# Second layer's keys of a two-layer encoder trunk: block turns on VectorE and 256-byte-run stores in place of transposes on TensorE

## The chip, the cores and the metric

One core of one Trainium2 chip runs the whole program in one launch. The metric is device time in microseconds (us); three runs of the kernel before give a median of 1708.25 us (1708.22 to 1708.37). The engines are TensorE (PE in the profile; PEld is its weight load), VectorE (DVE), ScalarE (ACT), GpSimd (POOL) and SyncE (SP). In this kernel POOL and SP mostly issue transfers.

## The reference

Two request groups, x_prompt and x_sample, of 512 tokens by 1024 numbers each, go through the same two layers: differential attention, then bidirectional retention, each with a SiLU gate and a residual, and a last norm. All is float32. What matters here is the second layer's mixer, cut to its core:

```python
def bidir_retention(h, w_in, decay_fwd, decay_bwd, subln_g, w_out):
    proj = h @ w_in
    q, k, v, gate = jnp.split(proj, [...], axis=-1)
    q = retention_rotate(q.reshape(B, S, N_HEADS, RET_QK_DIM))
    k = retention_rotate(k.reshape(B, S, N_HEADS, RET_QK_DIM)) * (RET_QK_DIM ** -0.5)
    log_g_f = -jnp.exp(decay_fwd)
    log_g_b = -jnp.exp(decay_bwd)
    o_f = retention_direction(q, k, v, log_g_f, True)
    o_b = jnp.flip(retention_direction(jnp.flip(q, 1), jnp.flip(k, 1), jnp.flip(v, 1), log_g_b, False), 1)
    o = rms_norm(o_f + o_b, subln_g, SUBLN_EPS)
    o = o.reshape(B, S, D_INNER) * jax.nn.silu(gate)
    return o @ w_out
# in retention_direction, for each chunk of tokens:
    scores = jnp.einsum('bqhd,bkhd->bhqk', qc, kc) * intra[None]
    state = (state * chunk_decay + jnp.einsum('bkhd,bkhe->bhde', kc * k_decay, vc))
```

There are 8 heads; a key of the second layer has 128 numbers, a value 256.

## The kernel before, in words

**Numbers.** A float32 operand is split into a high part (the float32r rounding, by ACT, `hi_of`, L534) and a low part (the rest, by DVE, `lo_of`, L537), and a product is three matmuls. The projections are done in blocks of seven products in place of eight (`Unit`, matmuls L752, and `Double`, for the values, with the operands changed over, matmuls L887; L1197 are the output projections').

**Stages.** Norm and first layer's projections, attention, its output projection, norm and second layer's projections (about 1060 to 1410 us of the span), retention (about 1410 to 1685 us), output projection, last norm. Both groups go through each stage. Between projections and mixers the rotated q and k, the values, the gates and the turned keys lie in HBM (`qk_d`, `v_d`, `g_d`, `kt_d`; qk, v, g and kt in the profile), stored by POOL's queue (L530) from the staging ring `os` and loaded by SP's queue.

**Keys of the second layer.** The projection leaves q and k with the head's 128 numbers along partitions and 512 tokens along the free axis. A unit holds a pair of heads. `rot_done` rotates its two halves into two tiles (an m and an e buffer), splits and stores them, and for keys calls `turn`, eight times in all (four pairs, two groups). The retention's state needs the keys the other way, tokens along partitions, multiplied by powers of the decay. `turn` (L968 to L993) turns each of the two tiles with four transposes on PE into a PSUM bank (L978, ring tp, one buffer), takes them out with two multiplies by `powers` (L982, DVE), and splits and stores two heads' keys of 512 KB each, high and low. In the retention, `fetch2` loads a block (one head of one group): q, k, values, turned keys (both parts, into the arena) and gate; L1784 are the state's products, of turned keys and values, twelve matmuls a block.

**What sets the order.** The program's operations are listed once, with what each reads and writes, in the class `Plan`; `arrange` puts them in an order by a list of costs and due times, per engine, and `issue` writes that order out. `SHIFTS` is a table of numbers, each row a place in time, a reach, a size, a share and a seed, which moves due times at random before each arrangement; so the table sets the order. Buffers come from rings: `os` 3, e 8, m 4, c 4, ws (split weights) 7; PSUM banks pj 3, sc 2, o 2, tp 1. An operation that writes a ring's next buffer waits for the last readers of the one before in that place, a store among them.

Of the kernel before, what the change touches and what calls it, by code (L numbers as in the profile page):

```python
# [10 lines left out]
F32 = mybir.dt.float32  # L11
# [71 lines left out]
class Buf:  # L83
# [37 lines left out]
    (1423.43, 30, 2, 0.05, 47590),
    (11.99, 16, 0.3, 0.05, 523605),
    (1423.39, 30, 1, 1, 258131),
    (542.13, 8, 2, 0.5, 679735),
    (11.49, 16, 0.3, 1, 785172),
    (1415.16, 30, 4, 0.05, 143263),
    (1052.6, 30, 2, 0.5, 712630),
    (1425.39, 30, 1, 0.5, 612061),
    (1421.39, 16, 2, 0.5, 937799),
    (1440.0, 16, 4, 0.2, 433253),  # L130
    (1432.0, 8, 2, 0.2, 226625),
    (1439.5, 16, 2, 0.5, 224311),
    (167.17, 30, 0.3, 1, 538302),
    (60.85, 8, 4, 0.2, 501862),
    (971.85, 16, 2, 0.2, 92752),
# [227 lines left out]
def trunk_kernel(  # L363
# [84 lines left out]
    def const(shape, tag, dt=F32, size=None):  # L448
        return Buf(plan, tag, 1, lambda i: view(cp, tag, i, size or math.prod(shape[1:]), shape, dt))
# [130 lines left out]
    powers = const([P, NH, NT], "powers")  # L580
# [344 lines left out]
    def rot_done(dst, tab, scaled, turned=None, weave=woven):  # L925
# [14 lines left out]
        def store(g, i, r):  # L940
# [29 lines left out]
        def turn(g, *r):  # L970
            h, to = turned
            out = [m_t("kt"), m_t("kt")]
            for i in range(2):
                tp = bank("tp", "ktp")

                def fn(i=i, tp=tp):
                    for t in range(NT):
                        nc.tensor.transpose(  # L978
                            tp[:, t * P:(t + 1) * P], unwoven(r[i].t)[:, t // 2, t % 2 * P:(t % 2 + 1) * P], ident.t)
                pe(0.44, fn, [r[i], ident], [tp], 2)  # L980
                for j in range(2):
                    dve(256, lambda i=i, j=j, tp=tp: nc.vector.tensor_tensor(  # L982
                        out[j].t.rearrange("p (t i c) -> p t i c", t=NT, i=2)[:, :, i, :],
                        tp.t.rearrange("p (t j c) -> p t j c", t=NT, j=2)[:, :, j, :],
                        powers[:, h + j, :].unsqueeze(2).broadcast_to([P, NT, 64]), op=ALU.mult),
                        [tp, powers], [(out[j], i)])
# [1031 lines left out]
```

## Time and profile before

| | |
|---|---|
| median of 3 runs | 1708.25 us |
| profiled execution's time | 1708.25 us |
| its span | 1706.5 us |
| PE busy | 1695.6 us (99%) |
| PEld busy | 1504.9 us (88%) |
| DVE busy | 1478.3 us (87%) |
| ACT busy | 906.1 us (53%) |
| POOL busy | 359.5 us (21%) |
| chain that ended last | PE 94%, DVE 4%, issue 1%, POOL 1% |

The span reaches from the first to the last instruction of the profiled execution; the time has 1.75 us more around it. In a group's row stand the line, the engine, the operation, output<-inputs by the program's names, shapes and count, then the busy time in us and the mean of one in ns, then the engine's idle time ahead of them and what ended it. In the waits a row names who waited for whom, us in total, times, and the longest. In the table of stretches the columns are the stretch, its length, then busy us and instructions of PE, PEld, DVE, ACT and POOL, the granted clock, the transfers' share and GB/s.

### The profile page before, as it was taken

The page shows a single profiled execution, that of the slowest core. Times are in us where ns is not written, and L with a number is a line of the kernel's source. Part 1 is how long each engine was busy: PE and PEld are TensorE (multiplying, and loading weights), DVE is VectorE, ACT ScalarE, POOL GpSimd, SP SyncE. Part 2 cuts the span into 40 slices and gives each one's busy share as a digit, 9 for nine tenths or more (in the row PEclk, how much of TensorE's full clock was granted, in tenths as well). Part 3 has the DMA queues.
Part 4 walks back from the last instruction along what each step waited for, and adds up shares of the span by engine and source line. Part 5 has one row for each costly group of instructions (what it writes and reads, how often), then busy time and mean ns, then how long its engine had stood idle before and what let it go on. Part 6 is the DMA issues. An engine that isn't in the chain of part 4 may idle for free.

```text
span 1706.5 us, 24879 instructions
## 1 busy us (share of the span) xinstructions
PE 1695.6 (99%) x8729; PEld 1504.9 (88%) x8729; DVE 1478.3 (87%) x2394; ACT 906.1 (53%) x1863; POOL 359.5 (21%) x656
## 2 busy tenths in 40 slices
PE   9999999999999999999999999999999999999998
PEld 8888888888888899888888988888888889999997
DVE  8978979989579889898888898877996797998988
ACT  8754444444444565555555876454544455544446
POOL 1111242222232212111111201124222321111114
PEclk9999999999999999999999999999999999999999
DMA  5344664556455795554443525456565569765652
GB/s 224 136 148 145 198 239 161 173 163 197 156 215 173 240 365 185 198 196 172 159 176 150 198 69 185 168 183 236 167 218 192 214 215 406 286 246 194 251 205 99
DMA packets 100469, 337.02 MB, mean 197 GB/s; under 512 B 14052, under 2 KB 15224, under 8 KB 100344
## 3 DMA queue, kind: packets, MB, share of 16 engines
q1 hardware_dynamic: 66992, 226.02, 36.7%
q0 software_dynamic: 33024, 109.08, 18.7%
q8 instruction: 68, 1.11, 0.3%
q14 instruction: 57, 0.47, 0.1%
q10 hardware_dynamic: 328, 0.34, 0.1%
HBM read 217.94 MB, written 117.44 MB: 197 GB/s over the span
## 4 chain that ended last, share of the span: by engine, by line
PE 94%; DVE 4%; issue 1%; POOL 1%; ACT 0%; DMA 0%; POOLq 0%; DVEq 0%; ACTq 0%
PE pj L752 20%; PE pj L1197 18%; PE sc L752 10%; PE o L752 8%; PE pj L887 7%; PE sc L1464 5%; PE o L887 4%; PE sc L887 4%; PE o L1538 3%; PE o L1805 3%; PE tp L887 2%; PE o L1585 2%; PE o L1813 1%; PE sc L1760 1%; PE tp L1784 1%; PE pj L1505 1%
## 5 line engine op out<-in xcount | busy, mean ns | idle before, releaser
L1197 PE MATMUL pj<-ws,arena 128*128 128x512 f32 x1542 | 359.1, 381 | 0.1
L1197 PEld LDWEIGHTS pj<-ws,arena 128*128 128x128 f32 x1542 | 283.9, 190 | 35.8 <-DVE m L1012 0.3
L752 PE MATMUL pj<-b,ws 128*128 128x512 f32 x1080 | 251.2, 380 | 1.1 <-DVE e L813 0.6
L752 PEld LDWEIGHTS pj<-b,ws 128*128 128x128 f32 x1080 | 203.5, 189 | 30.0 <-DVE e L813 1.0
L1203 DVE SCALAR_TENSOR_TENSOR b<-pj,pad,b 128x512 f32<-128x512 f32 (+1 forms) x257 | 190.1, 743 | 11.5 <-PE pj L1197 10.7
L537 DVE TENSOR_TENSOR ws<-raw,ws 128x512 fp32r<-128x512 f32 (+2 forms) x173 | 152.3, 884 | 41.9 <-PE tp L887 21.5
L530 POOL DMA_DIRECT2D qk<-os x192 | 102.3, 536 | 372.6 <-DVE os L537 304.4
L752 PE MATMUL sc<-arena,ws 128*128 128x512 f32 x768 | 177.2, 380 | 0.0
L537 DVE TENSOR_TENSOR ws<-st,ws 128x512 fp32r<-128x512 f32 (+1 forms) x184 | 138.7, 759 | 44.1 <-ACT ws L534 35.8
L534 ACT CAST ws<-st 128x512 fp32r<-128x512 f32 (+1 forms) x184 | 123.7, 675 | 97.7 <-PE pj L752 40.2
L534 ACT CAST ws<-raw 128x512 fp32r<-128x512 f32 (+2 forms) x173 | 133.8, 775 | 68.2 <-PE o L752 22.8
L752 PE MATMUL o<-arena,ws 128*128 128x512 f32 x744 | 169.2, 380 | 0.0
L752 PEld LDWEIGHTS sc<-arena,ws 128*128 128x128 f32 x768 | 144.8, 189 | 20.0
L752 PEld LDWEIGHTS o<-arena,ws 128*128 128x128 f32 x744 | 140.4, 189 | 19.7
L752 PE MATMUL pj<-arena,ws 128*128 128x512 f32 x636 | 148.7, 380 | 0.0
L752 PEld LDWEIGHTS pj<-arena,ws 128*128 128x128 f32 x636 | 120.3, 189 | 16.8
L530 POOL DMA_DIRECT2D v<-os x128 | 91.6, 717 | 149.2 <-DVE os L537 95.8
L1482 ACT ACTIVATE b<-sc,pad 128x512 f32<-128x512 f32 x128 | 87.2, 687 | 64.1 <-DVE pad L1472 64.1
L1472 DVE TENSOR_REDUCE pad<-sc 128x1 f32<-128x512 f32 x128 | 83.5, 684 | 4.2 <-PE sc L1464 4.1
L887 PE MATMUL pj<-ws,b 128*128 128x512 f32 x360 | 81.0, 379 | 0.0
L887 PEld LDWEIGHTS pj<-ws,b 128*128 128x128 f32 x360 | 68.2, 189 | 9.5
L805 ACT COPY c<-pj 128x512 f32<-128x512 f32 x72 | 42.0, 586 | 64.8 <-PE pj L752 60.0
(272 smaller groups left out, 3097.9 us busy)
## 6 DMA issues: line engine op xcount, KB each, us to landing
qk<-os POOLq DMA_DIRECT2D x192, 256.0 KB, 4.4
arena<-qk SPq DMA_DIRECT2D x80, 512.0 KB, 5.9
raw<-in_da_w_in_dram SPq DMA_DIRECT2D x71, 512.0 KB, 4.1
v<-os POOLq DMA_DIRECT2D x128, 256.0 KB, 2.8
arena<-v SPq DMA_DIRECT2D x64, 512.0 KB, 4.3
raw<-in_ret_w_in_dram SPq DMA_DIRECT2D x56, 512.0 KB, 4.1
os<-g SPq DMA_DIRECT2D x32, 512.0 KB, 9.1
g<-e POOLq DMA_DIRECT2D x48, 256.0 KB, 3.5
```

The lines of the kernel that those rows point to most:

```text
L530: plan.op(on, cost, lambda: q.dma_start(out(), in_()), r, w, lands=lands + kb / 200.0, kb=kb, load=any(isinstance(k[0] if isinstance(k, tu ...
L534: act(n, lambda: nc.scalar.copy(dst(), src()), r, w)
L537: dve(n, lambda: nc.vector.tensor_tensor(dst(), src(), hi().bitcast(F32), op=ALU.subtract), r, w)
L752: nc.tensor.matmul(ps.t, a[u][0]()[:, k, :], self.weave(bt[k][:, v, :]), start=(opens and k == 0 and i == 0), stop=(k == 3 and i == 2), sk ...
L887: nc.tensor.matmul(ps.t, bt[2 * kh + j][:, v, t * P:(t + 1) * P], woven(a[u][:, j, :]), start=(opens and kh + j + i == 0), stop=(kh == 1 a ...
L1197: nc.tensor.matmul(ps[:, here], o[a][:, e, t * P:(t + 1) * P], woven(u[b][:, e, :])[:, p * n // 2:(p + 1) * n // 2, :], start=(m == 0), st ...
L1203: axpy(n, lambda half=half, here=here, ps=ps: nc.vector.scalar_tensor_tensor(half, ps[:, here], rr[:, t % 2:t % 2 + 1], half, op0=ALU.mult ...
L1464: nc.tensor.matmul(s.t, q[:, a, t * P:(t + 1) * P], woven8(k[:, b, :]), start=(n == 0), stop=(n == 2))
L1472: dve(S, lambda s=s, m=m: nc.vector.tensor_reduce(m.t, s.t, op=ALU.max, axis=AX.X, negate=True), [s], [m])
L1482: act(840, lambda j=j, s=s, m=m: nc.scalar.activation(p[:, j, :], s.t, AF.Exp, bias=m.t, accum_out=sm[:, 2 * j + n:2 * j + n + 1]), [s, m] ...
L1538: nc.tensor.matmul(o.t, v[b][:, j, e * P:(e + 1) * P], woven(turned_aT(a)[:, j, :]), start=(n == 0), stop=(n == 11))
L1805: nc.tensor.matmul(o[:, e * 256:(e + 1) * 256], v_[v][:, 2 * c + j, e * P:(e + 1) * P], woven(a_[:, u, j * 256:(j + 1) * 256]), start=(e = ...
```

## The change

- `turn` no longer uses PE. Each of the two rotated tiles is turned by DVE in blocks of 32x32 (L994 of the changed kernel, STREAM_TRANSPOSE, 128x512) into halves of one os buffer; one DVE multiply by powers over 128x1024 (L996) follows. A block turn leaves the 32x32 blocks where they stand, so the places are put right by the stores: four per os buffer, each of 32 partitions with 16 runs of 64 numbers (256 bytes). A store moves 128 KB.
- For heads 0 and 1 the keys are split ahead of the stores (one 128x1024 cast on ACT, one 128x1024 subtraction on DVE, L1003), so eight stores a call; for the six other heads whole keys are stored, four stores a call. There are 40 of these stores where there were 16.
- `kt_d` holds tokens by numbers, `[2 or 1, 512, 128]`. `fetch2` loads it in runs of 512 bytes; for the six other heads it loads 256 KB into an e buffer and splits it there, ACT and DVE, a 128x512 operation each.
- The stores of rotated q and k of the second layer write their rows in another grouping (`quarters`), with runs as long as before.
- `powers` is four small tiles of 16 columns, computed by 16 DVE operations of 64x8 and four exponentials (before: two and one); `dec` moves from a constant to an e buffer.
- `SHIFTS` has 63 rows in place of 45, all others, so instructions stand in another order throughout. Line numbers grow by 18 or 19 (L752 is L770, L537 is L555, L530 is L548).

```diff
 SHIFTS = (
-    (69.47, 30, 2, 1, 966209),
...
+    (594.5, 30, 4, 1, 958469),
...
-    powers = const([P, NH, NT], "powers")
+    powers = [const([P, 16], f"powers{q}") for q in range(4)]
...
             for j in range(2):
-                dma(lambda j=j: dst[g][j, i * 64:(i + 1) * 64], lambda j=j: o[j * 64:(j + 1) * 64].bitcast(F32),
-                    [o], [(dst[g], (i, j))], 256, nc.gpsimd)
+                to = (lambda j=j: dst[g][j].rearrange("(x i y) u s -> i x y u s", x=2, i=2)[i]) if quarters else \
+                    (lambda j=j: dst[g][j, i * 64:(i + 1) * 64])
+                dma(to, lambda j=j: o[j * 64:(j + 1) * 64].bitcast(F32), [o], [(dst[g], (i, j))], 256, nc.gpsimd)
...
         def turn(g, *r):
             h, to = turned
-            out = [m_t("kt"), m_t("kt")]
+            o = os_t(F32, "kt")
+            rows = lambda: o.t.rearrange("p a s -> p (a s)")
             for i in range(2):
-                tp = bank("tp", "ktp")
-
-                def fn(i=i, tp=tp):
-                    for t in range(NT):
-                        nc.tensor.transpose(
-                            tp[:, t * P:(t + 1) * P], unwoven(r[i].t)[:, t // 2, t % 2 * P:(t % 2 + 1) * P], ident.t)
-                pe(0.44, fn, [r[i], ident], [tp], 2)
-                for j in range(2):
-                    dve(256, lambda i=i, j=j, tp=tp: nc.vector.tensor_tensor(
-                        out[j].t.rearrange("p (t i c) -> p t i c", t=NT, i=2)[:, :, i, :],
-                        tp.t.rearrange("p (t j c) -> p t j c", t=NT, j=2)[:, :, j, :],
-                        powers[:, h + j, :].unsqueeze(2).broadcast_to([P, NT, 64]), op=ALU.mult),
-                        [tp, powers], [(out[j], i)])
-            for j in range(2):
-                o, k = os_t(), out[j]
-                hi_of(S, lambda o=o, k=k: o[:, 0, :], lambda k=k: k.t, [k], [(o, 0)])
-                lo_of(S, lambda o=o: o[:, 1, :], lambda k=k: k.t, lambda o=o: o[:, 0, :], [k, (o, 0)], [(o, 1)])
-                dma(lambda j=j: to[h + j, g].rearrange("a p c -> p a c"), lambda o=o: o.t.bitcast(F32),
-                    [o], [to[h + j, g]], 512, nc.gpsimd)
+                dve(S + 150, lambda i=i: nc.vector.transpose(
+                    rows().rearrange("p (c i e) -> p i c e", c=16, i=2)[:, i], unwoven(r[i].t)), [r[i]], [(o, i)])
+            dve(2 * S, lambda: nc.vector.tensor_tensor(
+                rows().rearrange("p (c e) -> p c e", c=16), rows().rearrange("p (c e) -> p c e", c=16),
+                powers[h // 2].t.unsqueeze(2).broadcast_to([P, 16, 64]), op=ALU.mult), [o, powers[h // 2]], [o])
+            whole = [o]
+            if h == 0:
+                u = os_t(F32R, "kt")
+                hi_of(2 * S, lambda: u.t, lambda: o.t, [o], [u])
+                dve(2 * S, lambda: nc.vector.tensor_tensor(
+                    o.t.bitcast(F32R), o.t, u.t.bitcast(F32), op=ALU.subtract), [o, u], [o])
+                whole = [u, o]
+            for n, w in enumerate(whole):
+                for q in range(4):
+                    dma(lambda n=n, q=q: to[h + q // 2, g][n].rearrange("(c y) (x e) -> x y c e", y=32, x=2)[q % 2],
+                        lambda w=w, q=q: w.t.rearrange("p a s -> p (a s)")[32 * q:32 * q + 32].rearrange(
+                            "p (c e) -> p c e", c=16).bitcast(F32),
+                        [w], [(to[h + q // 2, g], (n, q % 2))], 200, nc.gpsimd)
         return done
...
-    kt_d = {(h, g): dram([2, P, NT * P], f"kt{h}{g}") for h in range(NH) for g in range(NG)}
+    kt_d = {(h, g): dram([2 if h < 2 else 1, S, P], f"kt{h}{g}") for h in range(NH) for g in range(NG)}
...
         t = kts[b] = slot(6 + b % 2, [P, 2, S], F32R, 36)
-        dma(lambda: t.t.bitcast(F32), lambda: kt_d[h, g].rearrange("a p c -> p a c"), [kt_d[h, g]], [t], 512)
+        parts = [(lambda n=n: t[:, n, :].bitcast(F32), (t, n)) for n in range(2)]
+        if h > 1:
+            k = e_t("kr")
+            parts = [(lambda: k.t, k)]
+        for n, (to, key) in enumerate(parts):
+            dma(lambda to=to: to().rearrange("p (t d) -> p t d", t=NT),
+                lambda n=n: kt_d[h, g][n].rearrange("(t p) d -> p t d", t=NT), [kt_d[h, g]], [key], 256)
+        if h > 1:
+            hi_of(S, lambda: t[:, 0, :], lambda: k.t, [k], [(t, 0)])
+            lo_of(S, lambda: t[:, 1, :], lambda: k.t, lambda: t[:, 0, :], [k, (t, 0)], [(t, 1)])
         sg[b] = load_sg(g_d[1, h, g])
```

**PE at the first turn.** In the order before, PE's instructions around the first call of `turn` (1088 to 1099 us in the trace) were these; o, sc, pj and tp are PSUM banks, ws split weights, arena and b operands that stay resident, m and e the two rotated tiles:

```order
L752 MATMUL o_293<-arena,ws_83 128x512 x12
L978 MATMUL tp_290<-ident_240,m_446 128x128 x4
L752 MATMUL sc_248<-arena,ws_85 128x512 x12
L752 MATMUL pj_357<-b_8350,ws_73 128x512 x3
L752 MATMUL pj_357<-b_8385,ws_73 128x512 x3
L752 MATMUL pj_357<-arena,ws_73 128x512 x6
L978 MATMUL tp_290<-ident_240,e_620 128x128 x4
```

In the changed order the same place reads:

```order
L770 MATMUL o_293<-arena,ws_83 128x512 x12
L770 MATMUL sc_248<-arena,ws_85 128x512 x12
L770 MATMUL pj_336<-b_8356,ws_73 128x512 x3
L770 MATMUL pj_336<-b_8389,ws_73 128x512 x3
L770 MATMUL pj_336<-arena,ws_73 128x512 x6
```

The two groups of four transposes are gone, and the products stand in the same succession.

**VectorE at the first turn.** Before, DVE took the turned keys out of the bank in four multiplies by powers (pad holds small tiles, powers among them), with a split of weights, rotations and sums of other units between, and split each head's keys into an os buffer:

```order
L537 TENSOR_TENSOR ws_83<-st_9075,ws_81 128x1024
L982 TENSOR_TENSOR m_250<-tp_290,pad_82 128x4x64
L982 TENSOR_TENSOR m_442<-tp_290,pad_82 128x4x64
L935 SCALAR_TENSOR_TENSOR m_446<-e_575,cos_1386 128x512
L935 SCALAR_TENSOR_TENSOR m_464<-pj_281,sin_1391 128x512
L813 TENSOR_TENSOR e_242<-o_293,c_524 128x512
L963 TENSOR_TENSOR m_446<-m_446,m_464 128x512
L852 TENSOR_TENSOR st_9191<-raw_268,raw_273 128x1024
L935 SCALAR_TENSOR_TENSOR e_575<-e_575,sin_1391 128x512
L852 TENSOR_TENSOR st_9075<-st_9075,raw_301 128x1024
L982 TENSOR_TENSOR m_250<-tp_290,pad_82 128x4x64
L982 TENSOR_TENSOR m_442<-tp_290,pad_82 128x4x64
```

In the changed order:

```order
L994 STREAM_TRANSPOSE os_372<-m_462 128x16x32
L1452 TENSOR_SCALAR pad_82<-pad_82,pad_78 64x8
L994 STREAM_TRANSPOSE os_372<-e_685 128x16x32
L555 TENSOR_TENSOR ws_83<-st_9074,ws_81 128x1024
L831 TENSOR_TENSOR e_520<-o_293,c_522 128x512
L870 TENSOR_TENSOR st_9169<-raw_268,raw_277 128x1024
L1452 TENSOR_SCALAR pad_82<-pad_82,pad_78 64x8
L555 TENSOR_TENSOR os_347<-e_685,os_347 128x512
L1452 TENSOR_SCALAR pad_82<-pad_82,pad_78 64x8
L982 TENSOR_TENSOR m_250<-m_250,m_445 128x512
L996 TENSOR_TENSOR os_372<-os_372,pad_82 128x1024
```

Both block turns now stand ahead of that weight split; the multiply by powers stands some operations later, with the tiny operations on powers between (L982 is here the subtraction of the rotation, L963 before).

**POOL at the first turns.** Before, the two heads' keys of a call were two stores of 512 KB, and the rotated queries' and keys' stores of 256 KB stood between the calls:

```order
L530 DMA kt_199<-os_363 128x2x512
L530 DMA kt_201<-os_608 128x2x512
L530 DMA qk_153<-os_348 64x1024 x2
L530 DMA qk_153<-os_363 64x1024 x2
L530 DMA kt_198<-os_608 128x2x512
L530 DMA kt_200<-os_348 128x2x512
```

In the changed order:

```order
L548 DMA kt_201<-os_608 32x16x64 x2
L548 DMA kt_199<-os_372 32x16x64 x2
L548 DMA kt_201<-os_372 32x16x64 x2
L548 DMA kt_199<-os_608 32x16x64 x2
L548 DMA qk_153<-os_347 2x32x1024 x2
L548 DMA qk_153<-os_372 2x32x1024 x2
L548 DMA kt_198<-os_347 32x16x64
L548 DMA kt_200<-os_347 32x16x64 x2
L548 DMA kt_198<-os_347 32x16x64
L548 DMA kt_200<-os_608 32x16x64 x2
L548 DMA kt_198<-os_608 32x16x64 x2
```

Each of the first two calls is now eight stores in a row, from two of the three os buffers, ahead of the next rotated tile's stores.

More of the change, by code (lines that the diff above doesn't have):

```diff
@@ L121 @@
[L121 to L135, printed above, removed]
@@ new lines @@
+    (612.92, 8, 1, 0.2, 825142),
+    (1295.36, 16, 4, 1, 196360),
+    (61.97, 4, 4, 1, 713104),
+    (609, 4, 2, 1, 211923),
+    (59.93, 8, 2, 1, 77292),
+    (1326.34, 8, 4, 0.5, 162340),
+    (1238.91, 8, 1, 1, 15893),
+    (1345.1, 30, 1, 0.5, 695733),
+    (61.09, 30, 2, 0.2, 90515),
+    (986, 30, 2, 0.5, 276758),
+    (56.98, 8, 2, 0.5, 715135),
+    (1414.46, 16, 4, 0.5, 299760),
+    (421.99, 8, 4, 0.5, 750152),
+    (1427.49, 8, 2, 0.2, 811151),
+    (988, 30, 1, 0.5, 812178),
+    (1430.57, 8, 0.3, 1, 408340),
@@ new lines @@
+    (1427.49, 8, 1, 0.5, 68685),
+    (1023.35, 16, 2, 1, 358065),
+    (53.97, 16, 0.3, 0.2, 339279),
+    (1436.0, 4, 1, 0.5, 525544),
+    (1327.78, 8, 1, 1, 47144),
+    (11.45, 30, 0.3, 1, 877137),
+    (1214.5, 16, 4, 1, 453551),
+    (1426.53, 30, 1, 0.5, 951220),
+    (1440.0, 8, 4, 0.5, 754746),
+    (1689.0, 8, 2, 0.5, 777090),
+    (1441.94, 30, 2, 0.05, 697582),
+    (594.5, 30, 4, 0.5, 933975),
+    (1197.91, 4, 1, 0.5, 134560),
+    (1246.06, 16, 0.3, 1, 248769),
+    (1425.82, 30, 2, 0.2, 132208),
@@ new lines @@
+    (1439.5, 16, 4, 0.05, 903428),
+    (1410.38, 16, 1, 0.2, 944937),
+    (145.11, 16, 4, 0.2, 518560),
+    (9.9, 4, 0.3, 0.2, 36223),
+    (302.74, 4, 2, 0.5, 676379),
+    (1266.75, 30, 1, 0.2, 834066),
+    (1427.34, 8, 4, 0.5, 560346),
+    (1422.32, 8, 1, 0.2, 647540),
+    (1410.14, 16, 4, 0.5, 957807),
+    (553.97, 16, 1, 0.05, 21125),
+    (1440.0, 4, 1, 0.2, 435068),
+    (1304.75, 30, 1, 1, 480905),
+    (338.95, 4, 1, 1, 115680),
+    (1255.02, 30, 2, 0.2, 752047),
+    (611.36, 8, 2, 0.5, 353769),
@@ new lines @@
+    (1455.0, 16, 2, 0.2, 137473),
+    (515.49, 16, 0.3, 0.5, 819485),
+    (1239.69, 8, 2, 0.5, 77142),
+    (49.93, 16, 1, 0.5, 653308),
+    (10.95, 8, 1, 0.5, 299928),
+    (1447.0, 4, 2, 0.5, 924328),
+    (44.64, 30, 0.3, 1, 831382),
+    (1439.5, 4, 1, 0.5, 71275),
+    (42.64, 30, 2, 0.2, 215811),
+    (1022.99, 8, 4, 1, 611074),
+    (27.45, 8, 2, 0.5, 829670),
+    (7.17, 16, 1, 0.05, 820394),
+    (547.13, 16, 2, 1, 13655),
+    (1021.47, 8, 2, 0.05, 657770),
+    (136.47, 4, 2, 1, 138735),
@@ L151 @@
+    (1116.47, 16, 1, 1, 945557),
 )
@@ L922, in evac, with rot_done @@
                 self.done(1, 0, X)
-    def rot_done(dst, tab, scaled, turned=None, weave=woven):
+    def rot_done(dst, tab, scaled, turned=None, weave=woven, quarters=False):
         cos, sin = tab
```

52 lines of the change are left out of this document (13 added, 39 removed).

## The prediction

> **What bounds the kernel now.** First the profile page's busy times, then the waits of TensorE (PE), then the chain of waits around a turn, then a table by stretch. A measurement of this kernel tells a difference from none at about 0.2%, 3.4 us.
>
> ```profile
> PE 1695.6 (99%) x8729; PEld 1504.9 (88%) x8729; DVE 1478.3 (87%) x2394; ACT 906.1 (53%) x1863; POOL 359.5 (21%) x656
> ```
>
> ```profile
> PE sc L1327 <- DVE pad L547: 1.2, 1, 1.2
> PE pj L752 <- DVE e L813: 0.6, 1, 0.6
> ...
> PE pj L752 <- DVE ws L537: 0.5, 1, 0.5
> ```
>
> PE is busy for 1695.6 of the span's 1706.5 us; its longest waits are the start's 1.2 us and two of half a microsecond. So the time is the length of PE's instruction sequence, plus the end. In the timeline PE's last row begins at 1689.69 and lasts 9.49:
>
> ```profile
> 1689.69 9.49 PE L1197 MATMUL pj<-ws,arena 128*128 128x512 f32 x49
> ```
>
> PE ends at 1699.18; 7.3 us of stores and norm follow. These steps are the same in both kernels, so whatever leaves PE's sequence leaves the span, as long as no other engine comes late. The chain of waits (start, duration, what), where the first two turns stand:
>
> ```profile
> 1087.93 2.16 PE o L752 x10
> 1090.09 0.46 PE tp L978 x4
> 1090.55 2.59 PE sc L752 x12
> ...
> 1095.74 0.47 PE tp L978 x4
> 1096.20 2.59 PE sc L752 x12
> 1098.79 2.59 PE pj L752 x12
> 1101.38 0.46 PE tp L978 x4
> 1101.85 1.30 PE sc L887 x6
> ...
> 1107.03 0.47 PE tp L978 x4
> ```
>
> Each group of four transposes takes 0.46 to 0.47 us of PE's sequence, with no gap to its neighbours: full price, nothing hides it.
>
> VectorE (DVE) is the engine that could take over. Stretches, with DVE's busy time in the third column of figures:
>
> ```profile
> 1090.00:1130.00 40.00, 40.00 (x193) 35.04 (x192) 38.36 (x53) 19.68 (x28) 10.13 (x18) 1.00 0.74 237
> 1130.00:1200.00 70.00, 70.00 (x327) 61.46 (x327) 48.48 (x71) 29.34 (x46) 24.20 (x35) 1.00 0.52 190
> 1200.00:1230.00 30.00, 30.00 (x146) 26.52 (x145) 30.00 (x53) 15.06 (x26) 7.64 (x13) 1.00 0.69 216
> ...
> 1260.00:1290.00 30.00, 30.00 (x146) 26.53 (x145) 30.00 (x44) 15.46 (x22) 6.74 (x12) 1.00 0.73 244
> ...
> 1360.00:1400.00 40.00, 40.00 (x194) 35.36 (x193) 39.93 (x69) 20.48 (x34) 10.03 (x17) 1.00 0.54 171
> 1400.00:1470.00 70.00, 70.00 (x441) 64.46 (x441) 58.49 (x99) 37.87 (x87) 13.35 (x23) 1.00 0.98 384
> ...
> 1500.00:1675.00 175.00, 175.00 (x1121) 161.34 (x1120) 156.94 (x263) 75.49 (x198) 21.93 (x40) 1.00 0.54 204
> ```
>
> The turns stand in four places, the stretches 1090:1130, 1200:1230, 1260:1290 and 1360:1400, and there DVE is 96 to 100% busy, while PE still never starves. So the change is worth what leaves PE, less what DVE, GpSimd (POOL) and the transfers then do too late in these four places. The granted clock is 1.00 throughout.
>
> **Part by part: what leaves PE.** The trace's records of the transposes, by operation (duration in ns, lowest/median/highest):
>
> ```profile
> L978 PE MATMUL tp<-ident,m x32: 271/282/285, 1089.9 to 1376.8; 128*128 128x128 f32 x32
> L978 PE MATMUL tp<-ident,e x32: 271/282/284, 1095.6 to 1382.4; 128*128 128x128 f32 x32
> ```
>
> 64 transposes, all alike, in 16 groups of four. A single one has 0.28 us from its start to its end, but they are pipelined: a group occupies 0.46 + 0.47 + 0.46 + 0.47 = 1.86 us per four groups, so 16 × 0.465 = **7.4 us** leaves PE. [...]
>
> **What DVE loses and gains.** DVE's own timeline in the first of these places (start, duration; an "x2" holds two):
>
> ```profile
> 1091.34 0.75 DVE L982 TENSOR_TENSOR m<-tp,pad 128x256 f32<-128x256 f32 x2
> 1092.00 0.70 DVE L935 SCALAR_TENSOR_TENSOR m<-e,cos 128x512 f32<-128x512 f32 x1
> ...
> 1093.83 0.68 DVE L963 TENSOR_TENSOR m<-m,m 128x512 f32<-128x512 f32 x1
> 1094.43 1.22 DVE L852 TENSOR_TENSOR st<-raw,raw 128x1024 f32<-128x1024 f32 x1
> 1095.56 0.70 DVE L935 SCALAR_TENSOR_TENSOR e<-e,sin 128x512 f32<-128x512 f32 x1
> ...
> 1099.71 1.28 DVE L537 TENSOR_TENSOR os<-m,os 128x512 fp32r<-128x512 f32 x2
> 1100.91 0.69 DVE L935 SCALAR_TENSOR_TENSOR m<-pj,cos 128x512 f32<-128x512 f32 x1
> ```
>
> From start to next start, a multiply by powers takes (1092.00 − 1091.34)/2 = 0.33 us, a 128x512 operation 0.60, a 128x1024 one 1.13, a low part into os 0.60. Per call of `turn` four multiplies and two low parts go: 4 × 0.33 + 2 × 0.60 = 2.52. In their place come two block turns at T each and one 128x1024 multiply: 2T + 1.13, and for heads 0 and 1 another 1.13 for the low part. The trace has no block turn. I bound T from below by a 128x512 operation, 0.61, and from above by a 128x1024 one, 1.22 us (each element handled twice), and take 0.61: the nearest row has the same elements, float32 from SBUF to SBUF. Then a call costs 2.35, for heads 0 and 1 3.48; over eight calls 6 × 2.35 + 2 × 3.48 − 8 × 2.52 = +0.9 us. With the other moved instructions, counted at these paces from the order, the queue of DVE is in 1200:1293 3.6 us shorter than before, where PE's is 3.7 shorter; ahead of the matmul at 1127 it is 2.2 shorter for PE's 1.9; and at the end of 1360:1400 between 0.6 and 4.2 shorter, against 1.9. About even, with a miss of up to 1.3 us in the last. I book **+0.3** for it.
>
> In the timeline, around 1127, six matmuls that take 1.30 in the chain take 1128.31 − 1126.76 = 1.55:
>
> ```profile
> 1126.76 1.71 PE L887 MATMUL pj<-ws,arena 128*128 128x512 f32 x6
> 1128.31 1.03 PE L887 MATMUL pj<-ws,b 128*128 128x512 f32 x4
> ```
>
> That small stall for split weights should go with DVE's shorter queue: **−0.25**.
>
> The splits of six heads' keys move to the retention stage. Its blocks, with 12 products of turned keys and values (L1784) each, are seen in this row's count:
>
> ```profile
> L1784 PE MATMUL tp<-arena x192: 272/275/276, 1411.0 to 1670.1; 128*128 128x256 f32 x192
> ```
>
> 16 blocks, and nearly 15 steps between the first and the last, so some 17.5 us a block. Twelve of them get +0.60 on DVE and one 128x512 cast on ScalarE (ACT). Ten steady blocks fill 1500:1675: 15.7 of 17.5 us on DVE, so 16.3 afterwards, and ACT from 7.5 to about 8.2. Covered, **0**; without the cover, 12 × 0.6 = 7.2 us, the whole gain. The powers become 16 tiny operations and four exponentials, under 2 us of DVE in all, within the counts above.
>
> **Stores on POOL.** Issue durations and landings (us from issue, last column of the second kind):
>
> ```profile
> L530 POOL DMA_DIRECT2D kt<-os x16 | 11.7, 734 | 42.5 <-DVE os L537 41.0 <-ACT ws L534 1.3 <-DVE m L935 0.2
> L530 POOL DMA_DIRECT2D v<-os x128 | 91.6, 717 | 149.2 <-DVE os L537 95.8 <-issue 34.5 <-ACT c L805 8.1
> L530 POOL DMA_DIRECT2D g<-e x48 | 26.9, 560 | 175.0 <-ACT e L1014 148.5 <-DVE e L1012 13.1 <-ACT c L805 6.2
> ```
>
> ```profile
> kt<-os POOLq DMA_DIRECT2D x16, 512.0 KB, 3.6
> ```
>
> Sixteen key stores at 0.73 us become forty with 512 runs each. Runs set the issue: g's 128 runs take 0.56, v's 256 take 0.72, 1.2 ns a run, so an estimated 0.717 + 256 × 1.23/1000 = 1.03 us for 512, with bounds 0.72 (bytes alone) and 2 × 0.734 = 1.47. Forty times 1.03 is 41 us instead of 12. POOL is busy 10 of 40 us in such stretches, so its sum doesn't matter; the bunch does. For heads 0 and 1 eight stores stand in a row, 8.2 us, and the rotated q/k stores behind them; both read the staging ring of three, which DVE's low parts and the block turns wait for. Booked **+0.3** for the two first turns; at 1.47 a bunch lasts 3.5 us longer, and both together would cost about 3.5 beyond the booked. [...] No run here shows a 256-byte store yet.
>
> **Loads.** In 1400:1470 transfers are busy 98% at 384 GB/s. The four loads of heads 0 and 1 there now move 512-byte instead of 4 KB runs. From nothing to as much again as their bytes take, 4 × 0.52 MB / 384 GB/s = 5.5 us; the later key loads halve, which helps. Four units of mostly covered time: **+0.25**. SP's queue gets seven more issues, and it is off the chain.
>
> **Start.** The order of the first 90 us is changed, with DVE at 45.00 of 45 us there:
>
> ```profile
> 15.00:60.00 45.00, 45.00 (x234) 39.66 (x233) 45.00 (x81) 37.29 (x69) 6.27 (x8) 1.00 0.39 148
> ```
>
> DVE's work up to there is the same in sum, so 0, ± 0.7.
>
> **Sum.** The profiled execution's time is 1708.25 with 1706.5 in the span; the median is 1708.25 too. 1708.25 − 7.4 − 0.25 + 0.3 + 0.3 + 0.25 = 1701.4 (rounded).
>
> **Rivals.** *Stores eat half.* Issue at the upper bound: 1701.4 + 3.5 = 1704.9, with its own range 1703.5 to 1707. For it: two uncertain prices (runs, and T up to the 0.78 that a low part into os reaches) meet in places where DVE is full. Against: POOL is idle three quarters there.
>
> *DVE's block turn is dear, and the kernel slower.* Place: the four full stretches. Sixteen turns at T instead of 0.61 cost 16 × (T − 0.61), of which some 1.6 us of idle DVE takes its share. At T = 1.22 that is 9.8 − 1.6 = 8.2, 1709.6: no difference. From T = 1.15 on the gain is gone, from T = 1.36 the kernel is measurably slower; at twice the dearest operation of this size, 1.56, it is 1701.4 + 15.2 − 1.6 = 1715. Against: every 128x512 row between SBUF tiles lies at 0.60 to 0.78. [...]
>
> *A transpose costs its whole record.* 64 × 0.28 = 17.9 instead of 7.4: 1690.9. The chain speaks clearly against it.
>
> *The new order also takes out waits.* PE's idle time ahead of its end is 10.9 − 7.3 = 3.6 us; without two thirds of it and with none of the losses: 1698.5.
>
> **How the numbers follow.** The forecast 1701.4 has 0.66 (own range 1699.5 to 1703.5); stores 0.17; dear block turn 0.06 without difference, 0.05 slower; whole record 0.01; order 0.05. Low end 1699.2 leaves out most of the last two; the high end 1706.2 takes in most of the stores' case and leaves out the dear turn: 0.2 outside. Faster by over 0.2% (below 1704.8): 0.66 + 0.06 + half of the stores' case, 0.08 = 0.80. Within: 0.09 + 0.06 = 0.15. Slower: 0.05.
>
> **What would show it.** Right: PE's busy time falls by 7 to 8 us, its waits stay near 3.6 us outside the end, block turns take 0.6 to 0.8, POOL's key stores about 1.0. Wrong: waits of PE on split weights or on e and c (DVE late) in the four places, DVE waiting for os behind POOL, PE waiting for L1784's keys near 1410, or a saving per group other than 0.465.

## The result and the profile after

The changed kernel takes 2252.5 us (median of 4 runs, 2250.7 to 2256.98) where the kernel before takes 1708.28: the ratio is 1.319, 95% interval 1.317 to 1.321. The forecast was 1701.4. It was wrong by 551 us, and on the wrong side.

The page's first part of the changed kernel, then two of its rows by slice (40 slices of 56 us: PE's busy tenths, and the granted clock in tenths):

```profile
PE 1749.8 (78%) x8665; PEld 1533.0 (68%) x8665; DVE 1485.5 (66%) x2398; ACT 901.4 (40%) x1864; POOL 382.2 (17%) x680
...
PE   9999999999999999999823384333343952399998
...
PEclk9999999999999999999966787766666976699999
```

No engine is full any longer. The instruction counts are as forecast (64 matmuls fewer), and VectorE's busy time rose by only 7.2 us. All the lost time lies in the 20th to the 35th slice, about 1100 to 1970 us: the second layer's projections, where the turns stand, and the start of the retention. PE waits there, and its clock falls to 0.6 to 0.8 of full speed in most of these slices; PE's busy time is 54 us longer with less work in it. PE's longest waits, then the longest of the engines behind them:

```profile
PE pj L770 <- DVE e L831: 83.5, 5, 31.1
PE sc L770 <- ACT c L823: 67.0, 3, 46.6
PE sc L905 <- DVE ws L555: 64.7, 4, 29.7
```

```profile
POOL qk L548 <- issue: 491.2, 58, 13.3
DVE os L555 <- ACT os L552: 431.0, 42, 40.3
ACT os L552 <- DMA qk<-os: 394.3, 21, 33.2
...
POOL kt L548 <- issue: 124.6, 36, 9.3
DVE os L994 <- DMA kt<-os: 89.7, 4, 46.0
```

PE waits for VectorE and ACT, and these for stores. Read from below: block turns wait for stores of keys, and ACT's high parts wait for stores of q and k, both for a place in the staging ring `os`; the stores wait on POOL for nothing that the profile shows ("issue"). POOL's timeline at the first turns (start, duration, and the idle time before):

```profile
1088.56 0.71 POOL L548 DMA_DIRECT2D qk<-os  x1 [15.56 <-DVE os L555]
1099.49 0.70 POOL L548 DMA_DIRECT2D qk<-os  x1 [10.22 <-issue]
1109.18 0.65 POOL L548 DMA_DIRECT2D qk<-os  x1 [8.99 <-issue]
1118.82 0.66 POOL L548 DMA_DIRECT2D qk<-os  x1 [8.99 <-issue]
1128.58 0.66 POOL L548 DMA_DIRECT2D kt<-os  x1 [9.09 <-issue]
1131.25 0.67 POOL L548 DMA_DIRECT2D kt<-os  x1 [2.01 <-issue]
1133.94 0.65 POOL L548 DMA_DIRECT2D kt<-os  x1 [2.02 <-DVE e L956]
```

Four stores of q and k that took 2.14 us to issue before now take 40 us: one every 9.8 us. The key stores follow at one every 2.67 us. The issue itself is short, 0.65 to 0.71 us for both, less than the 1.03 that was booked for the key stores. What is long is the time until POOL may issue again. The issues' list for 1080 to 1500 us (last column: us from issue to landing):

```profile
qk<-os POOLq DMA_DIRECT2D x28, 256.0 KB, 9.5
kt<-os POOLq DMA_DIRECT2D x24, 128.0 KB, 2.4
```

Landing and pace fit: each store is issued 0.3 us after the one before it has landed. In the kernel before, stores of the same 256 KB landed after 3.9 us and were issued every 0.54 us.

The records of the block turns have medians within the 0.6 to 0.8 us that the prediction named as a sign; the longest are above:

```profile
L994 DVE STREAM_TRANSPOSE os<-m x8: 711/712/872, 1089.3 to 1877.2; 128x512 f32<-128x512 f32 x8
L994 DVE STREAM_TRANSPOSE os<-e x8: 668/682/841, 1090.2 to 1877.8; 128x512 f32<-128x512 f32 x8
```

### The profile page after: what moved, and what is told of

The parts are those of the page before. It is cut to its first block, busy times and chain, and to the rows that moved or that the text cites. A ratio compares the mean times of both kernels' runs of the same rounds, so it can differ in the third digit from the quotient of the medians.

```text
span 2248.7 us, 24773 instructions
## 1 busy us (share of the span) xinstructions
PE 1749.8 (78%) x8665; PEld 1533.0 (68%) x8665; DVE 1485.5 (66%) x2398; ACT 901.4 (40%) x1864; POOL 382.2 (17%) x680
## 4 chain that ended last, share of the span: by engine, by line
PE 62%; issue 25%; DVE 5%; DMA 4%; POOL 3%; ACT 2%; POOLq 0%; ACTq 0%; SPq 0%; DVEq 0%
PE pj L1216 14%; PE pj L770 13%; PE sc L770 7%; PE o L770 6%; PE sc L1486 4%; PE pj L905 4%; DMA qk<-os 3%; PE o L1560 2%; PE sc L905 2%; PE o L1836 2%; PE o L905 2%; PE o L1607 1%; POOL qk L548 1%; PE tp L905 1%; DVE ws L555 1%
## 5 line engine op out<-in xcount | busy, mean ns | idle before, releaser
L770 PE MATMUL pj<-b,ws 128*128 128x512 f32 x1080 | 264.3, 394 | 131.4 <-DVE e L831 83.5
L1216 PE MATMUL pj<-ws,arena 128*128 128x512 f32 x1542 | 358.7, 381 | 0.0
L770 PEld LDWEIGHTS pj<-b,ws 128*128 128x128 f32 x1080 | 212.2, 198 | 166.4 <-DVE e L831 85.5
L548 POOL DMA_DIRECT2D qk<-os x192 | 110.7, 579 | 833.3 <-issue 491.2
L770 PE MATMUL sc<-arena,ws 128*128 128x512 f32 x768 | 181.2, 386 | 67.0 <-ACT c L823 67.0
L770 PEld LDWEIGHTS sc<-arena,ws 128*128 128x128 f32 x768 | 147.4, 193 | 89.5 <-ACT c L823 68.2
L555 DVE TENSOR_TENSOR os<-e,os 128x512 fp32r<-128x512 f32 x64 | 45.4, 711 | 232.3 <-ACT os L552 232.1
L555 DVE TENSOR_TENSOR ws<-raw,ws 128x512 fp32r<-128x512 f32 (+2 forms) x173 | 152.0, 881 | 29.8 <-ACT ws L552 15.9
L770 PE MATMUL o<-arena,ws 128*128 128x512 f32 x744 | 169.7, 380 | 0.3 <-DVE arena L615 0.3
L555 DVE TENSOR_TENSOR os<-m,os 128x512 fp32r<-128x512 f32 x64 | 45.3, 708 | 185.9 <-ACT os L552 185.6
L555 DVE TENSOR_TENSOR ws<-st,ws 128x512 fp32r<-128x512 f32 (+1 forms) x184 | 138.6, 756 | 39.3 <-ACT ws L552 33.8
L552 ACT CAST os<-m 128x512 fp32r<-128x512 f32 x64 | 45.0, 706 | 285.9 <-DMA qk<-os 163.4
L770 PEld LDWEIGHTS o<-arena,ws 128*128 128x128 f32 x744 | 140.7, 190 | 21.3 <-DVE arena L615 1.0
L552 ACT CAST os<-e 128x512 fp32r<-128x512 f32 x64 | 44.7, 698 | 260.8 <-DMA qk<-os 201.8
L770 PE MATMUL pj<-arena,ws 128*128 128x512 f32 x636 | 149.1, 380 | 0.0
L905 PE MATMUL sc<-ws,arena 128*128 128x512 f32 x288 | 79.8, 438 | 83.5 <-DVE ws L555 64.7
L905 PE MATMUL pj<-ws,arena 128*128 128x512 f32 x216 | 60.7, 436 | 98.2 <-DVE m L956 41.9
L770 PEld LDWEIGHTS pj<-arena,ws 128*128 128x128 f32 x636 | 120.7, 190 | 17.3
```

The source lines that it names most:

```text
L548: plan.op(on, cost, lambda: q.dma_start(out(), in_()), r, w, lands=lands + kb / 200.0, kb=kb, load=any(isinstance(k[0] if isinstance(k, tu ...
L552: act(n, lambda: nc.scalar.copy(dst(), src()), r, w)
L555: dve(n, lambda: nc.vector.tensor_tensor(dst(), src(), hi().bitcast(F32), op=ALU.subtract), r, w)
L770: nc.tensor.matmul(ps.t, a[u][0]()[:, k, :], self.weave(bt[k][:, v, :]), start=(opens and k == 0 and i == 0), stop=(k == 3 and i == 2), sk ...
L905: nc.tensor.matmul(ps.t, bt[2 * kh + j][:, v, t * P:(t + 1) * P], woven(a[u][:, j, :]), start=(opens and kh + j + i == 0), stop=(kh == 1 a ...
L1216: nc.tensor.matmul(ps[:, here], o[a][:, e, t * P:(t + 1) * P], woven(u[b][:, e, :])[:, p * n // 2:(p + 1) * n // 2, :], start=(m == 0), st ...
```

## The experiments

**Theory.** Two things hold POOL up. The regrouped q/k store has a leading dimension of 2 (2x32x1024), and by the theory only two of the 16 DMA engines then do its work: in the changed kernel's trace 52 of the 53 grouped stores that are alone in POOL's queue have, for most of the time, two packets of 4 KB under way. And POOL waits for landings: a grouped store is issued 0.30 us (median) after the grouped store before it has landed, and a key store 0.30 us after the key store before it. **Rivals.** The key stores' 256-byte runs are slow as such; or VectorE, with its block turns and the new order, is late.

The grouping alone, put into the kernel before (its keys then meet q rows in another order, so its output is another one):

```diff
-                dma(lambda j=j: dst[g][j, i * 64:(i + 1) * 64], lambda j=j: o[j * 64:(j + 1) * 64].bitcast(F32),
-                    [o], [(dst[g], (i, j))], 256, nc.gpsimd)
+                to = (lambda j=j: dst[g][j].rearrange("(x i y) u s -> i x y u s", x=2, i=2)[i]) if quarters else \
+                    (lambda j=j: dst[g][j, i * 64:(i + 1) * 64])
+                dma(to, lambda j=j: o[j * 64:(j + 1) * 64].bitcast(F32), [o], [(dst[g], (i, j))], 256, nc.gpsimd)
...
-                               (h, kt_d) if which else None))
+                               (h, kt_d) if which else None, quarters=True))
```

> The kernel before with nothing changed but the grouping of the second layer's 64 q/k stores (2x32x1024); rows of q and k then stand in another order than the turned keys' numbers, the work is the same. Two-engine theory: 64 stores at about 9.8 us from issue to next issue instead of 0.54, the four places of 16 stores each go from 40 us to about 160; 2100 to 2250 us. 256-byte theory: no such stores here, so 1708 within 5 us. Late-VectorE theory: 1708 within 5 us.

2174.69 us in a single run, 465.5 above the kernel before beside it (1709.15). It has no block turn, no short run and the old order, and shows the same waits:

```profile
POOL qk L530 <- issue: 478.6, 52, 13.6
ACT os L534 <- DMA qk<-os: 441.3, 29, 44.3
```

The packets of a grouped store can be counted on the two pages, of the kernel before and then of this one:

```profile
DMA packets 100469, 337.02 MB, mean 197 GB/s; under 512 B 14052, under 2 KB 15224, under 8 KB 100344
DMA packets 129141, 337.13 MB, mean 155 GB/s; under 512 B 42724, under 2 KB 43896, under 8 KB 129016
```

There are 28672 more packets under 512 bytes, 64 × 14 × 32. In the changed kernel's trace a grouped store that is alone in POOL's queue has 64 packets of 4 KB, never more than four of them at a time (30 of the 37 key stores that are alone there reach 16), and 464 = 14 × 32 + 16 packets of 4 bytes; POOL's 400 stores in the kernel before have 16 of these each, 6400. The trace names no DMA engine. The author's reading, which these counts fit, is that two DMA engines carry 32 runs each, the 14 others get as many tiny packets, and each of the 16 has one for the completion; counted so, a grouped store has 33 packets on every engine, also where it moves no data.

The other way round, the grouping taken out of the changed kernel, twice. In every kernel here that is made from the changed one, PE, VectorE and ACT run the changed kernel's instructions in the same succession; only the doubled turns (VectorE alone) and the mixed kernel differ. First with each grouped store made as two of 32 rows:

```diff
-                to = (lambda j=j: dst[g][j].rearrange("(x i y) u s -> i x y u s", x=2, i=2)[i]) if quarters else \
...
+                    for x in range(2):
+                        nc.gpsimd.dma_start(dst[g][j].rearrange("(x i y) u s -> i x y u s", x=2, i=2)[i, x],
+                                            o[j * 64 + x * 32:j * 64 + x * 32 + 32].bitcast(F32))
```

> The changed kernel, with each grouped 256 KB store of rotated q/k (2x32x1024) made as two stores of 32 rows each (32x1024), same order otherwise. Two-engine theory (a store is spread over as many DMA engines as its leading dimension, so 2x32x1024 runs on two; it takes 9.5 us and GpSimd can't issue the next until it has landed): each store lands in 2 to 4 us, GpSimd's qk waits go, and the time is 1700 to 1720 us; what stays are the key stores, one every 2.7 us. 256-byte theory (the key stores of 256-byte runs hold up GpSimd and the staging ring): still above 2100 us. Late-VectorE theory (block turns or the new order): still above 2100 us.

1758.09 us (ratio 1.029, 1.027 to 1.031): 494 us are gone, but not down to 1720, so the key stores were under-rated in that expectation. Then with the rows of before:

```diff
-                               (h, kt_d) if which else None, quarters=True))
+                               (h, kt_d) if which else None))
```

> The changed kernel with the q/k stores in the rows of before (64x1024, one dimension of 64 rows); q and k rows then stand in another order than the turned keys' numbers, so the retention's state product is another one, the work is the same. Two-engine theory: qk stores issue back to back in 0.54 us and land in 3 to 8 us as before; time 1700 to 1715 us. 256-byte theory and late-VectorE theory: still above 2100 us.

1755.87 us in a single run, the same within 3 us, again above the range. Both rivals are out as the main cause. POOL's timeline with the stores in two:

```profile
1096.19 1.93 POOL L967 DMA_DIRECT2D qk<-os  x4 [4.86 <-DVE pad L1456]
1099.61 0.69 POOL L548 DMA_DIRECT2D kt<-os  x1 [1.49 <-ACT os L552]
1103.88 0.66 POOL L548 DMA_DIRECT2D kt<-os  x1 [3.58 <-issue]
1106.56 0.66 POOL L548 DMA_DIRECT2D kt<-os  x1 [2.02 <-DVE ws L555]
...
1119.89 0.65 POOL L548 DMA_DIRECT2D kt<-os  x1 [2.01 <-issue]
1120.53 4.00 POOL L967 DMA_DIRECT2D qk<-os  x8
```

q/k now goes back to back, eight stores in 4.00 us, with 32 runs each: counted as above and shared evenly, two per DMA engine and one for the completion. The key stores still go one at a time: 512 runs each, counted so 32 per engine and one. Eight of them last 21 us; in this kernel ACT begins to fill an os buffer at 1102.7 and the next only at 1117.1.

Is it the leading dimension, or three dimensions as such? The same stores grouped 4x16x1024 and 8x8x1024:

```diff
-                to = (lambda j=j: dst[g][j].rearrange("(x i y) u s -> i x y u s", x=2, i=2)[i]) if quarters else \
+                to = (lambda j=j: dst[g][j].rearrange("(b i a) u s -> i a b u s", i=2, a=4)[i]) if quarters else \
```

> The changed kernel with the q/k stores grouped 4x16x1024 instead of 2x32x1024 (rows in another order than the turned keys' numbers, same bytes and runs of 4 KB). Two-engine theory, engines as many as the leading dimension: four engines move 16 runs each, 16 x 0.155 = 2.5 us of data instead of 5.0 and more, landing about 5 us after issue instead of 9.5; with 17 descriptors per engine three stores are under way at once, so an issue every 1.5 to 2 us; time 1760 to 1850 us. If the grouping itself (three dimensions) is what is slow, it lands at 9.5 us as before and stays above 2100.

> The changed kernel with the q/k stores grouped 8x8x1024 (rows in another order than the turned keys' numbers, same bytes, runs of 4 KB). Two-engine theory: eight engines, 8 runs of 4 KB and 9 descriptors each; landing near 4 us where nothing else runs (9.5 with a leading 2, about 6 with a leading 4, 2.9 to 3.6 with 64 rows), an issue every 0.6 us, seven under way at once; what is left is the key stores alone, so 1750 to 1765 us like the kernel with the stores in two. If the three-dimensional grouping costs by itself: well above that, 1800.

1795.81 and 1759.52 us, a single run each. The issues' lists in 1080 to 1500 us, leading 4, then leading 8:

```profile
qk<-os POOLq DMA_DIRECT2D x60, 256.0 KB, 6.2
```

```profile
qk<-os POOLq DMA_DIRECT2D x64, 256.0 KB, 4.4
```

From 9.5 through 6.2 and 4.4 to the 3.9 of 64 rows: the landing time falls with the leading dimension, at the same bytes and the same runs. So do the tiny packets: 27220 and 19028 under 512 bytes against 14932 with 64 rows, that is 64 × 12 × 16 and 64 × 8 × 8 more. With a leading 8 the grouping costs nothing that the split stores don't cost (1759.5 against 1758.1). That the packets fit 2, 4, 8 and 16 DMA engines at work is again the author's reading.

**The queue.** Key stores cut into halves of 16 partitions, 256 runs each, counted as above 16 per engine and one for the completion, with q/k still grouped:

```diff
-                    dma(lambda n=n, q=q: to[h + q // 2, g][n].rearrange("(c y) (x e) -> x y c e", y=32, x=2)[q % 2],
...
+                        for z in range(2):
+                            nc.gpsimd.dma_start(
+                                to[h + q // 2, g][n].rearrange("(c z y) (x e) -> x z y c e", z=2, y=16, x=2)[q % 2, z],
```

> The changed kernel with each 128 KB key store (32 partitions of 16 runs) made as two of 16 partitions each, q/k stores still grouped. [...] 256-byte theory: twice as many stores of the same runs, so as slow or slower, 2250 us and more.

2215.23 us in a single run, 37 below the changed kernel with twice as many stores of the same runs: short runs as such are not what costs. POOL's timeline there:

```profile
1129.67 1.70 POOL L1010 DMA_DIRECT2D kt<-os  x3 [8.48 <-issue]
1132.22 1.69 POOL L1010 DMA_DIRECT2D kt<-os  x3 [0.85 <-DVE ws L555]
1134.76 1.12 POOL L1010 DMA_DIRECT2D kt<-os  x2 [0.85 <-issue]
```

Three are issued together and the fourth waits: 3 × 17 = 51 fit, 68 don't. Two whole ones, 66, don't either. With a leading 8 the tightest case is seen, a key store and q/k stores of nine per engine by that count:

```profile
1119.94 0.65 POOL L548 DMA_DIRECT2D kt<-os  x1 [2.01 <-issue]
1120.58 1.69 POOL L548 DMA_DIRECT2D qk<-os  x3
1124.18 0.56 POOL L548 DMA_DIRECT2D qk<-os  x1 [1.92 <-issue]
```

33 + 3 × 9 = 60 fit, 69 don't. So the limit is at least 60 and below 66 per engine, if a store counts in full until it has landed, as the key stores' pace says (the next is issued 0.3 us after the landing, not before). That is an estimate from these issues and the count of runs; no trace shows the queue itself.

Both stores mended:

> The changed kernel with both kinds of second-layer stores split: q/k into two of 32 rows each, keys into halves of 16 partitions (17 descriptors per DMA engine). [...] Short-run theory (256-byte runs as such are slow to move): no better than 1758, since runs and bytes are the same.

1735.42 us (1.016, 1.014 to 1.017): 23 us better than with q/k alone, at the same runs and bytes, and 10 above the author's estimate of 1705 to 1725. The halves still come in bunches of 16; the first lasts from 1099.28 to 1114.32, 15 us where it was 21.

**What the rest is worth.** Keys stored as 64 partitions by 4 KB, counted as above five per engine, so that they reach the retention in another order; the work of the engines is the same:

```diff
+                        if q % 2 == 0:
+                            nc.gpsimd.dma_start(
+                                to[h + q // 2, g][n].rearrange("(p a) d -> p (a d)", a=8),
+                                w.t.rearrange("p a s -> p (a s)")[32 * q:32 * q + 64].bitcast(F32))
```

> The changed kernel with q/k split in two, and each head's keys stored as one plain store of 64 partitions by 4 KB (5 descriptors per DMA engine), so the keys reach the retention in another order of tokens and numbers; the work of TensorE, VectorE and ScalarE is the same. This takes both store troubles away and leaves the prediction's other steps: 1701.4, 1699 to 1704 us, if transposes were worth 0.465 us a group and VectorE keeps up. If VectorE (turns at 0.7 instead of 0.61, splits in the retention) or the new order costs more than booked: 1705 to 1712.

1707.1 us beside 1708.89 (0.999, 0.998 to 1.000). So the account closes: 2252.5 − 1758.1 = 494 for the grouping, 1758.1 − 1707.1 = 51 for the form of the key stores, and the rest of the change comes to −1.8. That the 51 are the queue's is seen in POOL's idle time ahead of key stores ended by "issue", here with q/k in two and then with both split; with 4 KB runs there is none:

```profile
POOL kt L548 <- issue: 77.4, 30, 5.4
POOL kt L1014 <- issue: 34.5, 34, 3.0
```

The busy times of the kernel with 4 KB runs and PE's waits:

```profile
PE 1690.7 (99%) x8665; PEld 1495.6 (88%) x8665; DVE 1489.2 (87%) x2398; ACT 909.4 (53%) x1864; POOL 384.8 (23%) x724
```

```profile
PE pj L770 <- DVE e L831: 1.5, 2, 1.0
PE sc L1352 <- DVE pad L565: 1.2, 1, 1.2
PE o L1842 <- DVE e L1860: 1.1, 2, 0.7
PE o L1842 <- ACT arena L552: 0.8, 1, 0.8
```

Where the forecast 7.4 us went is seen by comparing the end of the n-th matmul in both traces, the 64 transposes left out. At 90 us the new kernel is 1.6 late (the start); by 1062 it has won back half, and is 0.8 late. Over the four places of the turns it gains 2.0, 1.9, 0.6 and 1.9, where four groups are worth 1.86; the third place loses 1.0 to a product that waits for VectorE's e. At 1394 it is 5.4 ahead. By 1467 it is 1.2 ahead, and stays so to the end. So the retention's start takes back 4.2. The splits of the six heads' keys have no part in that: their first load into an e buffer is issued at 1454, and by 1445 nearly all is lost (1.3 ahead).

Do the 512-byte loads take them? The same kernel with plain loads in 2 KB runs:

```diff
-                lambda n=n: kt_d[h, g][n].rearrange("(t p) d -> p t d", t=NT), [kt_d[h, g]], [key], 256)
+                lambda n=n: kt_d[h, g][n].rearrange("(p a) d -> p (a d)", a=4), [kt_d[h, g]], [key], 256)
```

> As the kernel with keys in 4 KB store runs, with the key loads plain as well (128 partitions, runs of 2 KB instead of 512 bytes); keys again in another order, same work. It asks where the 4.2 us go that the kernel with 4 KB runs lost between 1394 and 1445. If the 512-byte runs of the first four blocks' loads take them (transfers there are 95% busy): 2 to 4 us faster than that kernel, 1703 to 1705. If it is the new order of the retention's start (products waiting for VectorE and ScalarE, little projection work left between them): within 1 us of it, 1706 to 1708.

1707.05 us, no change, and the same 4.2 us are lost. So the loads' runs aren't it. Its PE still waits there for ACT's and VectorE's operands:

```profile
PE o L1842 <- ACT arena L552: 2.2, 2, 1.4
```

And is VectorE as full as the windows said? Every block turn issued twice:

```diff
+                    for _ in range(2):
+                        nc.vector.transpose(
+                            rows().rearrange("p (c i e) -> p i c e", c=16, i=2)[:, i], unwoven(r[i].t))
```

> As the kernel with keys in 4 KB store runs, with every block turn issued twice, the same result: 16 x 0.6 = 9.8 us more on VectorE in the four places where it is full. By the prediction's rival 9.8 - 1.6 = 8.2 us slower than that kernel, 1715. If VectorE has more room there than its 96 to 100% say (its queue waits for ScalarE in part): 2 to 5 us slower, 1709 to 1712. If it isn't the limit at all: no change, 1707.

1717.13 us, 10.0 above the kernel with 4 KB runs. The busy times:

```profile
PE 1692.6 (99%) x8665; PEld 1495.9 (87%) x8665; DVE 1502.3 (88%) x2414; ACT 907.2 (53%) x1864; POOL 385.0 (22%) x724
```

VectorE has 1502.3 − 1489.2 = 13.1 us more, 0.82 a turn, and not the expected 9.8. Of these, 10.0 reach the time, and some 3 fall into its idle time. So VectorE is nearly the limit in these places, with a little room. In that run PE comes to the retention's start at 3.6 us behind the kernel before instead of 5.4 ahead, and loses 4.7 there, about as much. So it isn't a time fixed by transfers either, which would have given back the delay. What is left, by exclusion, is the new order of that stretch; which move in it costs was not tried.

**Other ways to the same keys.** Plain stores, with the places put right by four loads of 256-byte runs a key block:

```diff
+                for c in range(4):
+                    nc.sync.dma_start(
+                        to()[32 * c:32 * c + 32].rearrange("p (t x e) -> p t x e", t=NT, x=2),
+                        kt_d[h, g][n].rearrange("(x y) (t c e) -> c y t x e", x=2, t=NT, c=4)[c])
```

> As the kernel with keys in 4 KB runs, but the places are put right by the loads: four loads of 32 partitions with 256-byte runs a key block on SyncE's queue in place of one of 512-byte runs; the keys are the reference's again. [...] Short-run theory: the loads carry the cost instead, the retention's start waits for keys, over 1710.

1713.8 us (1.003, 1.002 to 1.004). The case over 1710 came: the loads aren't hidden in the retention's start, and the kernel is 6.7 us above the one with 4 KB runs, for which the author had estimated 2 at most. This kernel loses 11.7 us between 1394 and 1467, where the one with 4 KB runs loses 4.2, and PE waits for keys there:

```profile
PE tp L1826 <- DMA arena<-kt: 3.0, 2, 2.6
```

So heads 0 and 1, whose loads lie there, were given back to TensorE, with the six others turned as in the last kernel and a table of order of its own:

```diff
+            if h == 0:
+                out = [m_t("kt"), m_t("kt")]
+                for i in range(2):
+                    tp = bank("tp", "ktp")
...
+                return
```

> A mixed kernel with the reference's results: heads 0 and 1 as before (TensorE turns, 512 KB split stores, plain loads), heads 2 to 7 turned by VectorE, stored in 4 KB runs without being split, put right by four loads of 256-byte runs a block, which lie in the retention's even stretch; its q/k stores of 32 rows each; a table of order of its own. 12 of 16 groups of transposes are gone: 12 x 0.465 = 5.6 us. If the stretch 1400 to 1470 was hurt by key loads in short runs and their split, this leaves it as before: 1701 to 1705. If any order with the transposes gone meets loads there that can't come earlier: 1705 to 1709. If the 256-byte loads hold up the even stretch: above 1709.

1711.29 us (1.001, 1.000 to 1.002; single runs from 1708.5 to 1713.9). The profiled execution, 1713.93, is the slowest of its eleven. In it the four places gain 2.9 us where 5.6 were booked, and no wait of PE is on its keys' loads; but the retention's start takes 2.7 back, with heads 0 and 1 as before, and the kernel is 5.6 us behind already between 128 and 258 us, in the first layer, where three stores of q and k land after 9.5 to 9.7 us and a weight split comes late. The change has no part in that layer; whether the new table is the cause, or that one execution, no run separates. So the slow case of the expectation, above 1709, came without the cause that it names. No kernel tried here that computes the reference's keys is faster than the kernel before.

## Why the prediction was wrong, point by point

- **The edit that decided was given no price.** The prediction goes through the transposes, VectorE, the key stores, the loads and the start; the regrouped q/k stores appear in the description as "with runs as long as before" and in no term of the sum. They cost 494 us. Nothing was said of why they should be free but the run length. Run length and bytes were the same; the shape was 2x32x1024 instead of 64x1024, and it stood in the order's rows.
- **Landings had no price.** The sum has a term for the issue of the key stores and none for what waits on their landing. This step failed. A landing also decides when POOL can issue the next store: the grouped stores landed after 9.5 us and were issued every 9.8, the key stores after 2.4 and every 2.67. Its sign was in a row that the prediction quotes: the v stores of before, 256 runs each, have 34.5 us of idle time ended by "issue". In that trace three of them are under way together at 86 issues, and four at none; counted as above, 16 per engine and one, that puts the limit between 51 and 68.
- **Key stores.** The issue was estimated at 1.03 us with bounds 0.72 and 1.47; it is 0.66. The price was the wait behind it: 2.67 us from store to store. "POOL is busy 10 of 40 us, so its sum doesn't matter; the bunch does" named the right place, but priced the bunch of eight at 8.2 us; it lasts 21. Worth 51 us in all, where 0.3 was booked. The sign that the prediction named, "DVE waiting for os behind POOL", came; of its rivals, that of the stores named the place, at 3.5 us.
- **The 256-byte runs** as such explain none of the large loss: halves with the same runs were faster, not slower (2215.23 us against 2252.5), and with q/k in two the 128 KB key stores in 256-byte runs landed in 2.4 us where 128 KB of q/k in 4 KB runs took 3.1. The changed kernel's trace has 283 ns for a 4 KB packet of a key store against 159 for one of a q/k store, which the landing time doesn't show. What the short runs cost is, by the author's count, places in the queue, 32 per engine for 128 KB.
- **Transposes at 0.465 us a group.** Right: 1.9 to 2.0 us per four groups in three of four places. The rival of 0.28 us each was wrong. The sign that PE's busy time would fall by 7 to 8 us didn't show: it rose by 54 in the changed kernel, and fell by 4.9 with the store troubles away.
- **VectorE.** The block turn was bounded by 0.61 and 1.22, from start to next start, and taken at 0.61. By that measure it takes 0.77 in the mean in the kernel with 4 KB runs, 0.79 and 0.76 in the first call:

```profile
1089.97 0.86 DVE L998 STREAM_TRANSPOSE os<-m 128x512 f32<-128x512 f32 x1
1090.76 0.18 DVE L1458 TENSOR_SCALAR pad<-pad,pad 64x8 f32<-64x8 f32 x1
1090.86 0.83 DVE L998 STREAM_TRANSPOSE os<-e 128x512 f32<-128x512 f32 x1
1091.62 1.18 DVE L555 TENSOR_TENSOR ws<-st,ws 128x1024 fp32r<-128x1024 f32 x1
```

That is 16 × 0.16 = 2.6 us more than booked. The "miss of up to 1.3 us" came, 1.0, in the third place instead of the fourth. The rival's line, 16 × (T − 0.61) less 1.6 us of idle time, is right in kind: 13.1 us more on VectorE cost 10.0, so the idle time took 3.
- **Splits in the retention.** Right: from 1467 us on the kernel with 4 KB runs neither gains nor loses against before.
- **Retention's start and the first 90 us.** Booked 0.25 and 0 ± 0.7; measured 4.2 and 1.6, of which 0.8 is won back by 1062. The first is the second failed term of the sum. It was sought in the loads' runs, which a run has excluded; the order of that stretch is what is left, and which move in it costs stays open.

With the two store troubles away the sum would have been 1701.4 against a measured 1707.1: the mechanism was right and 6.3 of the 7.4 us were gained in the four places, but the retention's start and the first 90 us gave most of it back.

## What to carry to other kernels

Price every edit to a transfer by three numbers, not one: the bytes, the run, and the outermost dimension; here 256 KB in runs of 4 KB landed after 9.5 us with 2 and, in the kernel before, after 3.9 with 64. Count the runs of all stores in flight on one queue, and look for idle time ended by "issue" behind them; POOL, busy for 17% of the changed kernel's span, held up the other engines with 491 us of such idle time ahead of its q/k stores. A gain taken from the bounding engine in one place can be lost in the next, as here 4.2 us of 6.3 in the retention's start: follow the n-th instruction of that engine through both traces.

## What the runs showed of the hardware

A store of 256 KB in 64 runs of 4 KB landed in 9.5 us with a leading dimension of 2, 6.2 with 4, 4.4 with 8 and, in the kernel before, 3.9 with 64 rows. With a leading 2 the page has 28672 more packets under 512 bytes, with 4 12288 and with 8 4096. By the author's count of runs and completions, shared over 16 DMA engines, POOL's queue took 60 per engine, not 66. While PE waited for such stores its granted clock fell to 0.61 (1130 to 1200 us, in the table of stretches):

```profile
1130.00:1200.00 70.00, 17.11 (x55) 13.61 (x56) 21.05 (x26) 9.95 (x15) 9.92 (x15) 0.61 0.18 50
```

A 128x512 float32 block turn on VectorE had records of 0.67 to 0.87 us in the changed kernel, and 0.77 from start to next start in the mean of the kernel with 4 KB runs. In the changed kernel a 4 KB packet of a key store, in 256-byte runs, took 283 ns in the median, one of a q/k store, in a single run, 159; 128 KB of such keys still landed in 2.4 us.
